# A decoder block in float32: the gate and up products of its SwiGLU by one level of Strassen's scheme

## The chip, the cores and the metric

The kernel runs on one core of one Trainium2 chip. The metric is the device time of one execution in microseconds (us), median of the runs. TensorE (PE) multiplies, VectorE (DVE), ScalarE (ACT) and GpSimd (POOL) do the elementwise work, SyncE (SP) issues every transfer between device memory and the on-chip memory SBUF; TensorE writes its products into PSUM, eight banks of 128 x 512 numbers.

## The reference

One decoder block over 1024 tokens of width 1024, all in float32:

```
mix = [norm(attention) | norm(pooling)] @ w_out
h   = x + norm(mix)
hn  = norm(h)                                              # 1024 x 1024
ff  = (silu(hn @ w_gate) * (hn @ w_up)) @ w_down           # 1024 -> 2816 -> 1024
h   = h + norm(ff)
out = h + sigmoid(h @ w_ple_gate) * norm(p @ w_ple)
```

The change concerns `hn @ w_gate`, `hn @ w_up`, and the work right before and after them.

## The kernel before

**Split operands.** Every factor of a large product is held as two parts, `hi + lo`, each of 12 significant bits. `split` (L102) makes them: ScalarE casts to `hi` (L104), VectorE subtracts to get `lo` (L105). `mm3` (L107) then issues three matmuls for each block of 128 x 128 by 128 x 512: hi by hi (L110), hi by lo (L111), lo by hi (L112).

**Order.** The kernel is written in Tile: buffers come from pools, a planner puts the instructions of each engine in an order by its own timing model, within the dependences, and places the semaphores. An instruction that waits holds back everything behind it on its engine. SP's queue is in order too. A pool lies at the left or the right end of SBUF's partitions (`side="right"`); pools of one side are stacked.

**The stages, in order.** Embedding, norm and the v projection (0 to 100 us); pooling mixer, q and k projections, attention (100 to 385 us); then the output projection: `pooled(t)` and `mixed(t)` for each of eight token tiles, and `rest(t)` (L579), which adds the residual, stores h, takes the second norm and transposes the tile into `h2T` (left side, hi and lo parts of 8 x 128 x 1024). Behind the last tiles, three products on the first half of the tokens run ahead (`early`, L601).

**The loop over the hidden width.** 2816 columns are 22 tiles of 128, in 11 chunks of two. For each tile, `ff_weights` loads 1024 x 128 of w_gate and w_up (512 KB each, pool `wg`, right side) and splits them; `ff_product` (L564) multiplies them with one half of the tokens, 8 blocks by 3 matmuls = 24 matmuls into one PSUM bank; `ff_half` (L620) takes Silu of the gate, multiplies it by up and splits the result (`f`, right side). When a chunk's two tiles are there, the down product runs over all eight token tiles and both halves of the output width, 96 matmuls, with the split rows of w_down (right side), and is added to `acc` by VectorE (L676). The next chunk follows.

**The end.** In the last chunk the loads and splits of w_ple_gate (`wpg`, left side) and the load of the last norm's gain into the one buffer `wd_raw` are issued. `hidden(t)` (L641) makes the norm of `acc`, adds it to h and transposes; `gated(t)` (L681) multiplies by `wpg` and writes the output.

## Time and profile before

| | us |
|---|---|
| median of 3 runs (1307.39 to 1310.54) | 1307.99 |
| span of the profiled execution, first to last instruction | 1305.0 |
| TensorE busy in it | 1279.1 |
| VectorE, ScalarE, GpSimd busy | 575.1, 421.0, 124.4 |

The profile gives a span and no time of its own execution; the span lies 3.0 us below the median of the runs. In the timeline a row has start, duration, engine, line, operation and the buffers written and read; the bracket at its end tells for how long the engine had been idle before it and what ended that. A matmul's duration (0.39 us) contains its way through the array, and the next one begins before it ends: the pace is the distance of two starts.

### The profile page before, as it was taken

What the parts mean: (1) busy time and instruction counts of PE and PEld (TensorE: products, weight loads), DVE (VectorE), ACT (ScalarE), POOL (GpSimd) and SP (SyncE); (2) the same over time, 40 slices, a digit from 0 to 9 for tenths busy, and PEclk for the clock granted to TensorE, in tenths of its full rate; (3) what the DMA queues carried; (4) which work ended last, traced back from release to release, by engine and by line L of the source; (5) the groups of instructions that cost most, each with busy time, mean ns of one, the idle gap of its engine ahead of it and who ended that gap; (6) DMA issues with size and microseconds to landing.
All of it is one profiled execution on the core that took longest, in us unless ns stands there. A gap on an engine that the chain in (4) does not pass through costs nothing.

```text
span 1305.0 us, 15784 instructions
## 1 busy us (share of the span) xinstructions
PE 1279.1 (98%) x6228; PEld 1051.4 (81%) x6228; DVE 575.1 (44%) x958; ACT 421.0 (32%) x790; POOL 124.4 (10%) x197
## 2 busy tenths in 40 slices
PE   8999999998999999999999999999999999998998
PEld 6898878887887878888888888888888888887887
DVE  6544635567674553133343333342424242417443
ACT  6533525567674543311111111212120212015211
POOL 2210200000014330000000000000000000007210
PEclk9999999999999999999999999999999999999999
DMA  9632495468515533111212121111111211124331
GB/s 301 213 101 74 151 278 152 137 192 229 139 36 186 159 104 97 48 51 34 63 33 65 33 65 33 53 44 50 36 62 33 65 33 54 44 68 142 105 121 65
DMA packets 107770, 128.77 MB, mean 99 GB/s; under 512 B 7792, under 2 KB 83376, under 8 KB 107696
## 3 DMA queue, kind: packets, MB, share of 16 engines
q1 hardware_dynamic: 107696, 127.76, 32.1%
q8 instruction: 49, 0.80, 0.3%
q14 instruction: 25, 0.20, 0.1%
HBM read 98.35 MB, written 29.39 MB: 98 GB/s over the span
## 4 chain that ended last, share of the span: by engine, by line
PE 89%; DMA 5%; ACT 2%; DVE 2%; issue 1%; POOL 1%; SPq 0%; DVEq 0%; ACTq 0%; POOLq 0%
PE ps_F L110 11%; PE ps_F L111 11%; PE ps_F L112 11%; PE ps_A L110 10%; PE ps_A L112 10%; PE ps_A L111 10%; PE ps_T L111 3%; PE ps_T L110 3%; PE ps_T L120 3%; PE ps_T L112 3%; PE ps_O L111 3%; PE ps_O L110 3%; PE ps_O L112 3%; PE ps_O L468 1%; PE ps_A L427 1%
## 5 line engine op out<-in xcount | busy, mean ns | idle before, releaser
L110 PE MATMUL ps_A<-h2T,wg_hi 128*128 128x512 f32 x352 | 139.0, 395 | 0.2 <-ACT h2T L104 0.2
L111 PE MATMUL ps_A<-h2T,wg_hi 128*128 128x512 f32 x352 | 138.8, 394 | 0.0
L110 PE MATMUL ps_F<-h2T,wg_hi 128*128 128x512 f32 x352 | 138.8, 394 | 0.0
L112 PE MATMUL ps_A<-h2T,wg_lo 128*128 128x512 f32 x352 | 138.7, 394 | 0.0
L112 PE MATMUL ps_F<-h2T,wg_lo 128*128 128x512 f32 x352 | 138.7, 394 | 0.0
L111 PE MATMUL ps_F<-h2T,wg_hi 128*128 128x512 f32 x352 | 138.7, 394 | 0.0
L623 DVE TENSOR_TENSOR sg<-ps_F,sg 128x512 f32<-128x512 f32 x44 | 30.4, 690 | 179.4 <-PE ps_F L112 179.4
L104 ACT CAST wd_hi<-wd_raw 128x1024 fp32r<-128x1024 f32 x22 | 23.1, 1051 | 251.1 <-PE ps_O L112 215.5
L104 ACT CAST wg_hi<-wg_raw 128x1024 fp32r<-128x1024 f32 x44 | 46.2, 1049 | 156.8 <-issue 77.9
L105 DVE TENSOR_TENSOR wg_lo<-wg_raw,wg_hi 128x1024 fp32r<-128x1024 f32 x44 | 55.6, 1263 | 84.3 <-ACT wg_hi L104 81.5
L676 DVE TENSOR_TENSOR acc<-ps_T,acc 128x512 f32<-128x512 f32 x80 | 55.2, 690 | 76.1 <-PE ps_T L112 76.0
L110 PEld LDWEIGHTS ps_A<-h2T,wg_hi 128*128 128x128 f32 x352 | 65.9, 187 | 16.4 <-ACT h2T L104 0.5
L111 PEld LDWEIGHTS ps_A<-h2T,wg_hi 128*128 128x128 f32 x352 | 65.9, 187 | 16.4 <-DVE h2T L105 0.4
L112 PEld LDWEIGHTS ps_F<-h2T,wg_lo 128*128 128x128 f32 x352 | 65.8, 187 | 16.3
L111 PEld LDWEIGHTS ps_F<-h2T,wg_hi 128*128 128x128 f32 x352 | 65.8, 187 | 16.2
L110 PEld LDWEIGHTS ps_F<-h2T,wg_hi 128*128 128x128 f32 x352 | 65.8, 187 | 16.2
L112 PEld LDWEIGHTS ps_A<-h2T,wg_lo 128*128 128x128 f32 x352 | 65.9, 187 | 16.1
L105 POOL TENSOR_TENSOR wpg<-wg_raw,wpg 128x1024 fp32r<-128x1024 f32 x3 | 7.4, 2471 | 703.8 <-ACT wpg L104 703.8
L676 DVE TENSOR_TENSOR acc<-ps_O,acc 128x512 f32<-128x512 f32 x80 | 55.2, 690 | 42.9 <-PE ps_O L112 42.8
L110 PE MATMUL ps_O<-wd_hi,f 128*128 128x512 f32 x176 | 68.6, 390 | 0.4 <-DVE acc L676 0.4
L111 PE MATMUL ps_T<-wd_lo,f 128*128 128x512 f32 x176 | 69.0, 392 | 0.0
L110 PE MATMUL ps_T<-wd_hi,f 128*128 128x512 f32 x176 | 68.7, 390 | 0.0
(265 smaller groups left out, 2813.2 us busy)
## 6 DMA issues: line engine op xcount, KB each, us to landing
wg_raw<-in_w_ffn_gate_dram SPq DMA_DIRECT2D x22, 512.0 KB, 4.0
wg_raw<-in_w_ffn_up_dram SPq DMA_DIRECT2D x22, 512.0 KB, 3.9
wd_raw<-in_w_ffn_down_dram SPq DMA_DIRECT2D x22, 512.0 KB, 3.6
xt<-in_x_dram SPq DMA_DIRECT2D x16, 512.0 KB, 5.0
wc_raw<-in_w_in_dram SPq DMA_DIRECT2D x12, 512.0 KB, 5.9
ed<-eo SPq DMA_DIRECT2D x8, 512.0 KB, 3.6
vd<-vs SPq DMA_DIRECT2D x8, 512.0 KB, 3.2
qs<-qd SPq DMA_DIRECT2D x8, 512.0 KB, 5.3
```

The costliest lines, as they stand in the source:

```text
L104: nc.scalar.copy(hi, raw)
L105: lo_by.tensor_tensor(out=lo, in0=raw, in1=hi.bitcast(F32), op=ALU.subtract)
L110: nc.tensor.matmul(ps, lh, rh, start=first, stop=False)
L111: nc.tensor.matmul(ps, lh, rl, start=False, stop=False)
L112: nc.tensor.matmul(ps, ll, rh, start=False, stop=last)
L120: nc.tensor.transpose(tp[:, j * P:(j + 1) * P], src[:, (c + j) * P:(c + j + 1) * P], ident)
L427: nc.tensor.matmul(ps[:, 0:n], qs[:, tok(i)], kh[:, c0:c1_], start=True, stop=False)
L468: nc.tensor.matmul(po[:, q0:W2], vh[:, j, :], pTs[1][:, j, q0:W2], start=False, stop=j == nj - 1)
L623: nc.vector.tensor_tensor(out=sg, in0=up, in1=sg, op=ALU.mult)
L676: nc.vector.tensor_tensor(out=acc[:, t, half(hf)], in0=ps, in1=acc[:, t, half(hf)], op=ALU.add)
```

## The change

The products A^T h for a gate or up weight are done on pairs of hidden tiles. A weight of 1024 x 256 is cut into quarters (two halves of the 1024 rows, two tiles of 128 columns), the transposed norm into quarters (two halves of the rows, two halves of the tokens), and the four quarter results come from seven products of quarters in place of eight, after Winograd's form of Strassen's scheme: four sums of weight quarters (S1 to S4, on GpSimd), four sums of token quarters (T1 to T4, made once), and seven sums of results, of which four are made by accumulating in PSUM and three by VectorE.

- One product of quarters is 4 blocks by 3 matmuls = 12 matmuls. There are 22 weights (`q`), 11 gate and 11 up, of seven products each.
- `rest(t)` no longer makes `h2T`. For tokens 0 to 511 it keeps both halves raw (`rw`) and splits them (B11, B21); for tokens 512 to 1023 it forms the differences on VectorE and GpSimd and splits B22. T1 to T4 are split after the last tile.
- Weights that meet B11, B21 and B22 (left side) lie on the left, in the place of the attention's result (`wl`); those that meet T1 to T4 (right side) lie on the right (`wr`, 4 buffers). For the first two weights all lie on the right.
- A weight pair is one load of 1 MB into one of two buffers (`wide`); the first two products (`first_two`) of the next weight are placed ahead of the last product of this one.
- The SwiGLU result is stored to a device buffer `ffd`, not kept. After the whole phase a second loop reads it back by 128 rows with w_down, splits both (pool `fd`, in the place of T1 to T4), and does the same down products as before. `wpg` and the gain `gfp` are loaded in that loop's third chunk and at its beginning.

```diff
-            transposed(tt, h2T[0][:, :, tok(t)], h2T[1][:, :, tok(t)], KT, "O")
+            if t < 4:
+                for c, name in enumerate(("B11", "B21")):
+                    nc.scalar.copy(rw[:, c, :, cols], tps[c])
+                    split(tps[c], hq[name][0][:, :, cols], hq[name][1][:, :, cols])
+            else:
+                r0, r1, r2, r3 = (rw[:, i, :, cols] for i in range(4))
+                nc.vector.tensor_tensor(out=r2, in0=tps[0], in1=r0, op=ALU.subtract)
+                nc.vector.tensor_tensor(out=r3, in0=tps[1], in1=r2, op=ALU.subtract)
+                split(tps[1], hq["B22"][0][:, :, cols], hq["B22"][1][:, :, cols])
+                nc.gpsimd.tensor_tensor(out=r0, in0=r3, in1=r0, op=ALU.subtract)
+                nc.gpsimd.tensor_tensor(out=r1, in0=r1, in1=r3, op=ALU.subtract)
...
-        ws = [ff_weights(w_gate, 0), ff_weights(w_up, 0), ff_weights(w_gate, 1)]
-        early = [ff_product(w, 0, tag) for w, tag in zip(ws, "AFA")]
...
+    psum_layout(Q=8)
...
+    def weights(raw, left):
+        a11, a21 = raw[:, 0:K2, 0:P], raw[:, 0:K2, P:2 * P]
+        a12, a22 = raw[:, K2:KT, 0:P], raw[:, K2:KT, P:2 * P]
+        def summed(x_, y_, op):
+            s = swp.tile([P, K2, P], F32, name="sw")
+            nc.gpsimd.tensor_tensor(out=s, in0=x_, in1=y_, op=op)
+            return s
+        out = {"A11": quarter_w(a11, left), "A12": quarter_w(a12, left)}
+        yield out
+        s1 = summed(a21, a22, ALU.add)
+        out["S1"] = quarter_w(s1, False)
+        s2 = summed(s1, a11, ALU.subtract)
+        out["S2"] = quarter_w(s2, False)
+        s4 = summed(a12, s2, ALU.subtract)
+        out["S4"] = quarter_w(s4, True)
+        s3 = summed(a11, a21, ALU.subtract)
+        out["S3"] = quarter_w(s3, False)
+        out["A22"] = quarter_w(a22, False)
+        yield out
...
+    def first_two(q):
+        q["a"], q["b"] = bank("Q"), bank("Q")
+        product(q["a"], q["w"]["A11"], "B11", True)
+        product(q["b"], q["w"]["A12"], "B21", True)
+
+    def middle(q):
+        a, b, w = q["a"], q["b"], q["w"]
+        p1 = temp()
+        nc.scalar.copy(p1, a)
+        c11 = temp()
+        nc.vector.tensor_tensor(out=c11, in0=b, in1=p1, op=ALU.add)
+        c = bank("Q")
+        product(c, w["S1"], "T1", True)
+        p5 = temp()
+        nc.scalar.copy(p5, c)
+        product(a, w["S2"], "T2", False)
+        u2 = p1
+        nc.scalar.copy(u2, a)
+        product(c, w["S4"], "B22", False)
+        c12 = u2
+        nc.vector.tensor_tensor(out=c12, in0=c, in1=u2, op=ALU.add)
+        product(a, w["S3"], "T3", False)
+        c22 = p5
+        nc.vector.tensor_tensor(out=c22, in0=a, in1=p5, op=ALU.add)
+        q["c"] = [c11, c12, None, c22]
+
+    def last(q):
+        product(q["a"], q["w"]["A22"], "T4", False)
+        q["c"][2] = q["a"]
...
+    for n in range(EARLY):
+        start(n)
+        first_two(qs[n])
+    for i, name in ((2, "T1"), (3, "T2"), (0, "T3"), (1, "T4")):
+        for k in range(0, K2, 2):
+            split(rw[:, i, k:k + 2, :], hq[name][0][:, k:k + 2, :], hq[name][1][:, k:k + 2, :])
+    lt = h2pool.tile([P, 16, HALF], F32, name="lt", tag="rw")
+    for n in range(NQ):
+        if n + 1 < NQ and n + 1 >= len(qs):
+            start(n + 1)
+        next(qs[n]["gen"])
+        middle(qs[n])
+        if n + 1 < NQ and n + 1 >= EARLY:
+            first_two(qs[n + 1])
+        last(qs[n])
+        if n % 2 == 0:
+            finish_gate(qs[n])
+        else:
+            finish_up(qs[n - 1], qs[n], n // 2)
...
+        def split_rows(f):
+            raw = wg.tile([P, 2, D], F32, name="fd_raw", tag="wide", bufs=2)
+            nc.sync.dma_start(out=raw[:, 0, :], in_=w_down[tok(f), :])
+            nc.sync.dma_start(out=raw[:, 1, :], in_=ffd[tok(f), :])
...
+            made = [split_rows(f) for f in range(f0, f0 + CHUNK)]
+            if f0 == 2 * CHUNK:
+                for k in range(0, KT, 2):
+                    raw = wg.tile([P, 2, D], F32, name="wpg_raw", tag="wide", bufs=2)
+                    nc.sync.dma_start(out=raw, in_=w_pg[k * P:(k + 2) * P, :].rearrange("(j q) c -> q j c", q=P))
+                    split(raw, wpg[0][:, k:k + 2, :], wpg[1][:, k:k + 2, :])
```

Here EARLY is 3, NQ is 22, K2 is 4, and `quarter_w` splits one quarter of a weight (4 x 128 columns) into hi and lo. `finish_gate` takes Silu of the four quarter results, `finish_up` multiplies them and stores them to `ffd`, 256 KB each.

## Rows read from the trace of the kernel before

**Rows 1.** The page: busy time, share of the span, instructions of TensorE
```profile
PE 1279.1 (98%) x6228; PEld 1051.4 (81%) x6228; DVE 575.1 (44%) x958; ACT 421.0 (32%) x790; POOL 124.4 (10%) x197
```

**Rows 2.** Windows: stretch, busy (count) of PE, PEld, DVE, ACT, POOL; clock; DMA; GB/s
```profile
620.00:800.00 180.00, 180.00 (x780) 145.74 (x779) 63.13 (x82) 27.66 (x36) 0.00 (x0) 1.00 0.16 47
1170.00:1206.00 36.00, 32.83 (x140) 25.79 (x138) 23.84 (x27) 17.42 (x25) 22.10 (x16) 0.95 0.42 146
1206.00:1305.00 99.00, 94.86 (x460) 77.99 (x460) 39.79 (x55) 20.50 (x36) 18.91 (x13) 1.00 0.29 96
```

**Rows 3.** Timeline of TensorE: first down matmul, second and eleventh chunk
```profile
577.38 0.39 PE L110 MATMUL ps_T<-wd_hi,f 128*128 128x512 f32 x1
...
1177.14 0.39 PE L110 MATMUL ps_T<-wd_hi,f 128*128 128x512 f32 x1
```

**Rows 4.** Timeline of TensorE: two gate/up matmuls, 24 matmuls apart
```profile
560.35 0.39 PE L112 MATMUL ps_A<-h2T,wg_lo 128*128 128x512 f32 x1
...
565.95 0.39 PE L112 MATMUL ps_F<-h2T,wg_lo 128*128 128x512 f32 x1
```

**Rows 5.** Timeline of TensorE: two matmuls of an input projection, 24 apart
```profile
109.59 0.39 PE L110 MATMUL ps_F<-hT,wc_hi 128*128 128x512 f32 x1
...
115.03 0.39 PE L110 MATMUL ps_A<-hT,wc_hi 128*128 128x512 f32 x1
```

**Rows 6.** Timeline of TensorE: two matmuls of the embedding, 5 apart
```profile
61.06 0.39 PE L110 MATMUL ps_F<-wpp,pT 128*128 128x512 f32 x1
...
62.19 0.39 PE L112 MATMUL ps_F<-wpp,pT 128*128 128x512 f32 x1
```

**Rows 7.** Groups by form, 500 to 1170 us: busy us, mean ns, idle before
```profile
L676 DVE TENSOR_TENSOR acc<-ps_T,acc 128x512 f32<-128x512 f32 x72 | 49.7, 691 | 76.0 <-PE ps_T L112 76.0
...
L105 DVE TENSOR_TENSOR wg_lo<-wg_raw,wg_hi 128x1024 fp32r<-128x1024 f32 x39 | 47.8, 1226 | 81.7 <-ACT wg_hi L104 79.2
...
L104 ACT CAST wg_hi<-wg_raw 128x1024 fp32r<-128x1024 f32 x39 | 40.9, 1049 | 150.0 <-issue 77.9 <-PE ps_A L111 72.1
...
L105 DVE TENSOR_TENSOR f<-sg,f 128x512 fp32r<-128x512 f32 x41 | 28.3, 689 | 15.1 <-ACT f L104 15.1
...
L104 ACT CAST f<-sg 128x512 fp32r<-128x512 f32 x41 | 25.4, 620 | 93.1 <-DVE sg L623 93.1
...
L622 ACT ACTIVATE sg<-ps_A 128x512 f32<-128x512 f32 x40 | 23.8, 595 | 52.2 <-PE ps_A L112 52.2
...
L674 ACT COPY acc<-ps_T 128x512 f32<-128x512 f32 x8 | 4.7, 588 | 9.8 <-PE ps_T L112 9.8
```

**Rows 8.** Groups by form, 400 to 485 us: the residual addition on GpSimd
```profile
L585 POOL TENSOR_TENSOR xt<-xt,pb 128x1024 f32<-128x1024 f32 x8 | 19.2, 2396 | 11.6 <-DVE pb L584 9.8 <-DMA xt<-in_x_dram 1.8
```

**Rows 9.** Timeline of ScalarE, 560 us: the copy behind the product of rows 4
```profile
560.84 0.60 ACT L622 ACTIVATE sg<-ps_A 128x512 f32<-128x512 f32 x1 [4.24 <-PE ps_A L112]
```

**Rows 10.** Timeline of VectorE and GpSimd around 457 us: two instructions that meet
```profile
457.47 2.87 DVE L105 TENSOR_TENSOR wg_lo<-wg_raw,wg_hi 128x1024 fp32r<-128x1024 f32 x1
...
456.85 2.41 POOL L585 TENSOR_TENSOR xt<-xt,pb 128x1024 f32<-128x1024 f32 x1 [1.40 <-DVE pb L584]
```

**Rows 11.** Timeline around 480 us: last token tile's norm, its transposes, the next product
```profile
478.23 1.27 DVE L588 SCALAR_TENSOR_TENSOR pb<-xt,h_r,gfr 128x1024 f32<-128x1024 f32 x1
...
481.08 1.03 PE L120 MATMUL ps_O<-ident,pb 128*128 128x128 f32 x8
482.36 0.50 PE L110 MATMUL ps_A<-h2T,wg_hi 128*128 128x512 f32 x1 [0.24 <-ACT h2T L104]
```

**Rows 12.** DMA issues: size of each, median us from issue to landing
```profile
wg_raw<-in_w_ffn_gate_dram SPq DMA_DIRECT2D x22, 512.0 KB, 4.0
```

**Rows 13.** Timeline around 1197 us: last down product, start of the gate
```profile
1196.19 1.28 DVE L648 SCALAR_TENSOR_TENSOR dn<-acc,y_r,wd_raw 128x1024 f32<-128x1024 f32 x1 [2.56 <-DMA wd_raw<-in_g_ffn_post_dram]
...
1197.33 0.39 PE L112 MATMUL ps_T<-wd_hi,f 128*128 128x512 f32 x1
...
1206.57 0.48 PE L112 MATMUL ps_A<-wpg,h 128*128 128x512 f32 x1
```

More of the change, by code (lines that the diff above doesn't have):

```diff
@@ L497, in block_kernel, with wide, narrow @@
     woa = pool(o_ctx, "woa", side="right")
-    wobs = [[wg.tile([P, D], F32R, name=f"wob{i}{k}", tag="wg_raw" if k == 3 else ("wg_hi", "wg_lo")[i],
-                     bufs=2 if k == 3 else 3) for k in range(4)] for i in range(2)]
+    def wide(name, bufs=2):
+        return wg.tile([P, 2, D], F32R, name=name, tag="wide", bufs=bufs)
+    def narrow(name):
+        return wg.tile([P, D], F32R, name=name, tag="wr", bufs=4)
+    wob01 = [wide(f"wob{k}") for k in range(2)]
+    wob23 = [[narrow(f"wob{i}{k}") for k in (2, 3)] for i in range(2)]
+    wobs = [[wob01[0][:, i, :], wob01[1][:, i, :], wob23[i][0], wob23[i][1]] for i in range(2)]
     woas = [woa.tile([P, 4, D], F32R, name=f"woa{i}") for i in range(2)]
@@ L554, in block_kernel, with quarter @@
     psum_layout(A=2, F=2, T=2, O=2)
-    def ff_weights(w, f):
-        raw = wg.tile([P, KT, P], F32, name="wg_raw", bufs=2)
-        nc.sync.dma_start(out=raw, in_=w[:, tok(f)].rearrange("(k q) c -> q k c", q=P))
-        hi = wg.tile([P, KT, P], F32R, name="wg_hi")
-        lo = wg.tile([P, KT, P], F32R, name="wg_lo")
-        split(raw, hi, lo)
-        return hi, lo
-    def ff_product(w, hf, tag):
-        ps = bank(tag)
-        for k in range(KT):
-            mm3(ps, (w[0][:, k, :], w[1][:, k, :]), (h2T[0][:, k, half(hf)], h2T[1][:, k, half(hf)]), k == 0, k == KT - 1)
-        return ps
+    K2 = KT // 2
+    hq = {}
+    def quarter(p, name):
+        hq[name] = [p.tile([P, K2, HALF], F32R, name=f"{name}{i}") for i in range(2)]
     h2_ctx = ExitStack()
     h2pool = pool(h2_ctx, "h2pool")
-    h2T = [h2pool.tile([P, KT, S], F32R, name=f"h2T{i}") for i in range(2)]
+    rw = h2pool.tile([P, 4, K2, HALF], F32, name="rw", tag="rw")
+    for name in ("B11", "B21", "B22"):
+        quarter(h2pool, name)
     with ExitStack() as c1:
@@ new lines, in block_kernel, with quarter_w @@
+    ffd = dram.tile([FF, S], F32, name="ffd")
+    psum_layout(Q=8)
+    g1_ctx = ExitStack()
+    cright = pool(g1_ctx, "cright", side="right")
+    swp = pool(g1_ctx, "swp", 5)
+    for name in ("T1", "T2", "T3", "T4"):
+        quarter(cright, name)
+    wl = apool.tile([P, 4, 2, K2, P], F32R, name="wl", tag="a_sb")
+    nl = [0]
+    def quarter_w(src, left):
+        if left:
+            w = wl[:, nl[0] % 4]
+            nl[0] += 1
+        else:
+            w = wg.tile([P, 2, K2, P], F32R, name="wr", tag="wr", bufs=4)
+        split(src, w[:, 0], w[:, 1])
+        return w
@@ new lines, in product, with temp @@
+    def product(ps, w, name, first):
+        for k in range(K2):
+            lh, ll, rh, rl = w[:, 0, k, :], w[:, 1, k, :], hq[name][0][:, k, :], hq[name][1][:, k, :]
+            for i, (l, r) in enumerate(((lh, rh), (lh, rl), (ll, rh))):
+                nc.tensor.matmul(ps, l, r, start=first and k == 0 and i == 0, stop=k == K2 - 1 and i == 2,
+                                 skip_group_check=not first)
+    late = [0]
+    def temp():
+        i = late[0] % 16
+        late[0] += 1
+        return lt[:, i, :]
@@ new lines, in last, with finish_gate, finish_up @@
+    def last(q):
+        product(q["a"], q["w"]["A22"], "T4", False)
+        q["c"][2] = q["a"]
+    def finish_gate(q):
+        q["sg"] = []
+        for i in (0, 1, 3, 2):
+            sg = q["c"][i] if i != 2 else temp()
+            nc.scalar.activation(out=sg, in_=q["c"][i], func=AF.Silu)
+            q["c"][i] = sg
+    def finish_up(g, u, f):
+        for i in (0, 1, 3, 2):
+            o = g["c"][i]
+            nc.vector.tensor_tensor(out=o, in0=u["c"][i], in1=g["c"][i], op=ALU.mult)
+            r0 = (2 * f + i // 2) * P
+            nc.sync.dma_start(out=ffd[r0:r0 + P, half(i % 2)], in_=o)
@@ new lines, in block_kernel, with start @@
+    NQ = 2 * (NF // 2)
+    EARLY = 3
+    qs = []
+    def start(n):
+        gen = weights(load_pair((w_gate, w_up)[n % 2], n // 2), n > 1)
+        q = {"w": next(gen), "gen": gen}
+        qs.append(q)
+    for n in range(EARLY):
[5 more added lines that the diff above has]
+    lt = h2pool.tile([P, 16, HALF], F32, name="lt", tag="rw")
```

117 lines of the change are left out of this document (51 added, 66 removed).

## The prediction

> **What bounds the kernel now.** I read the page first: TensorE is busy for 1279.1 of 1305.0 us [rows 1]. Busy time hides short stalls, since a matmul of 0.39 us overlaps its successor, so the windows by stage and then single distances come next. From 620 to 800 us TensorE is busy all the time and the other engines at most a third of it, GpSimd never [rows 2]. The loop has one rhythm: from the second to the eleventh chunk's first down matmul, nine chunks, 599.76 us pass [rows 3], 66.64 each. A chunk has 4 weights x 2 halves x 24 = 192 gate/up matmuls and 96 down matmuls. Two gate/up matmuls 24 apart lie 5.60 us apart [rows 4]: 0.2333 us each, 44.80 for 192. The remaining 21.84 give 0.2275 for a down matmul. So the loop is matmul pace and nothing else: only fewer or closer matmuls shorten it, and other engines' work is free while TensorE never waits for it.
>
> **The two paces.** In gate/up the weights lie on the right side, `h2T` on the left. In down both factors lie on the right, as in the input projections, where 24 matmuls take 5.44 us, 0.2267 each [rows 5]. In the embedding both lie on the left: five distances, 1.13 us, 0.226 [rows 6]. So either side alone is fast, the mixture slow. The Trainium skill ("TensorE: Matmul & The Clock Gate", Step-by-step: what each phase is for) says that TensorE has two independent read ports, so loading weights does not slow the running matmul. By that rule placement would be worth nothing. [rows 4 to 6] show 0.0066 us per matmul.
>
> **What the change takes away.** Gate/up loses 22 tiles x 96 = 2112 matmuls x 0.2333 = 492.8 us. It gets 22 weights x 7 products x 12 = 1848 matmuls. At 0.2275, the down pace, which I choose because there too splits and additions run alongside, that is 420.4; the first two weights meet B11, B21 and B22 across the sides, 72 matmuls x 0.0058 = 0.4. Saved: 492.8 - 420.8 = **72.0 us**. Bounds: 73.5 if all run at 0.2267; 61.6 if placement did nothing here and all ran at 0.2333 (431.2).
>
> **What the phase costs beside TensorE.** One weight is 84 x 0.2275 = 19.1 us of TensorE. ScalarE: seven quarter casts of 128x512 at 0.620, three PSUM copies at 0.588, half of four Silus at 0.595 [rows 7] = 7.3 us. VectorE: seven subtractions at 0.689, three result sums and half of four products at 0.691 [rows 7] = 8.3 us. GpSimd: four sums, half of 2.396 each [rows 8] = 4.8 us. All are covered by 19.1. GpSimd and VectorE can meet: the subtraction at 457.47 us took 2.87 us, while GpSimd added until 459.26 [rows 10], against 1.226 alone [rows 7]. The Trainium skill ("SBUF — State Buffer", Who interferes with whom) has VectorE instructions with two SBUF inputs block against GpSimd ones that read SBUF; the row agrees. If each of the four sums blocks one subtraction for its whole length, VectorE has 13.1 us, still below 19.1.
>
> The narrow place is PSUM. S2 T2 accumulates into the bank that the copy p1 reads, S4 B22 waits for the copy p5, S3 T3 for u2, and A22 T4 for the sum c22. p5 and u2 have one product, 12 x 0.2275 = 2.73 us, to hide in. The copy behind the product of [rows 4] began 0.10 us after its last matmul's end (560.35 + 0.39) [rows 9]; that matmul ends 0.16 us after the next could start. With 0.59 for the copy and 0.2 for the way back to TensorE (a guess: the 0.10 of the way there, doubled) about 1.05 us pass; 1.7 us are left for whatever stands ahead in ScalarE's queue, two casts. p1 and c22 have more (three and two products). I take 2 us in all; bounds 0 and 26 (1.2 us a weight).
>
> Loads: 1 MB a weight. 512 KB land in 4.0 us [rows 12]; twice that is 8. A `wide` buffer comes free when A22 two weights before is split, eleven products (30 us) before the data is needed, so this is covered. If not, the next `first_two` is late. The stores to `ffd` add 11.5 MB to SP's queue behind loads that wait; the 16 temporaries last over two weight pairs.
>
> **The start.** In before, the three early products, 72 matmuls or 16.8 us, fill the wait for the last token tile's norm: it ends at 479.5, its transposes start at 481.08, and the next product at 482.36 with 0.24 us lost [rows 11]. In after, the third weight's load must wait for the first weight's buffer, which is read until its A22 split, and that waits for a `wr` buffer that S1 T1 still reads. So only two weights, 48 matmuls, can run ahead: 5.6 us of cover are gone. Behind the transposes, T1 needs a subtraction (0.69), a cast of 1024 (1.05) and its subtraction (1.23) [rows 7], about 3.2 us with handovers where before 0.5 passed: 2.7. The GpSimd differences of the tiles before (2 x 1.2) can stand in front of that norm's GpSimd steps: 0 to 2.4, I take 1. The first weight's last product has no `first_two` ahead of it, so c22 shows: 1.1. Sum 10.4; I take 10. Bounds: 3, if products fill the gaps, and 18, if T2 to T4 (six more subtractions of 1.23 on VectorE) come in sequence as well.
>
> **The turn to down.** c22 shows again at the last weight (1.1). The f rows' lo parts lie where T4 lay, so two subtractions of 1.23 start only after the very last product, perhaps behind `finish_up`'s last product of 0.69. I take 4; bounds 2 and 10 (if the reading of `ffd` also waited for the last stores: a store and a load, some 4 us each by [rows 12]).
>
> **Down.** Per chunk TensorE 21.84; VectorE 16 x 0.691 + 4 x 1.226 = 16.0, GpSimd nothing. In the third chunk four `wpg` splits add 9.8 to VectorE, more than the chunk's room, but the next chunk has 5.8 spare and four PSUM banks buffer. I take 1; bounds 0 and 5.
>
> **The end.** In before, from 1197.33 to 1206.57 us [rows 13] TensorE does 7 down matmuls, 12 transposes (0.1 each) and 4 gate matmuls, 3.6 us of work in 9.2: 5.6 lost, while the gain's late load ends VectorE's wait at 1196.19 [rows 13] and the clock averages 0.95 [rows 2]. With `wpg` and gain there long before, the first `hidden` can run in the last chunk. I take a gain of 4.5; bounds 0 and 5.6. The rest of the gate stage keeps its sides and its pace.
>
> **The sum.** 1305.0 - 72.0 + 2 + 10 + 4 + 1 - 4.5 = 1245.5 us of span; plus the 3.0 us by which the runs' median lies above this profile's span: **1248 us**. All bounds at their best: 1305.0 - 73.5 + 0 + 3 + 2 + 0 - 5.6 + 3.0 = 1234.
>
> **Rivals.**
> 1. *The PSUM handovers bind.* ScalarE's queue is in order; a cast that waits for a late GpSimd sum holds up p5 or u2 behind it. For: GpSimd's instructions do meet VectorE's [rows 10]. Against: 7.3 of 19.1 us on ScalarE, and 1.7 us of room. Between 0.5 and 2 us a weight: 1257 to 1290.
> 2. *The same place, on the other side.* If p5, u2 and c22 all come late, each by 0.9 us more than its cover, a weight loses 2.7 us, 22 weights 59 us, and the time is about 1305: same; above that, slower. The point is 2.7 us a weight. For ScalarE to cause it, it must be 2.6 us late at p5 and u2 each time, with 62% of its time free; hence unlikely. At 3.5 us a weight: 1323.
> 3. *Placement does nothing.* If something else than the sides sets the pace, and all 1848 matmuls run at 0.2333 [rows 4], the time is 1248 + 431.2 - 420.8 = 1258. Against: three stages show the pairing [rows 4 to 6], none another one. The Trainium skill's two read ports speak for it, as said.
> 4. *The borders cost more.* Start and turn at their upper bounds together: +8 and +6, with a lower clock after longer idling: about 1263.
>
> **How the numbers follow.** The forecast (1236 to 1256) has 0.58, rival 1 0.14, rival 2 0.07 (0.03 of it same, 0.04 slower), rival 3 0.08, rival 4 0.10, and something better than 1236 0.03. 1248 is the likeliest case. For 8 in 10 the range reaches from the best bounds, 1234, to 1278: it holds the forecast, rivals 3 and 4 and the milder part of rival 1. Faster by over 0.3% (below 1304; 0.3% is about what a measurement here tells from no change): 0.93; within 0.3%: 0.03; slower: 0.04.
>
> **What would show it.** Right: 84 matmuls a weight at 0.2267 to 0.2283 us, weights 19.1 to 19.3 us apart, TensorE idle only at the start (some 10 us), the turn (4) and the end; the down chunks 21.9 us apart. Wrong: weights 20 us or more apart with TensorE released by ScalarE's copies; a pace of 0.2333; idle time before the products of the third weight or in the third down chunk.

## The result and the profile after

The changed kernel takes **1274.35 us** (median of 4 runs, 1271.23 to 1277.43) against 1307.69 us (1305.92 to 1310.54) for the kernel before on the same chip: ratio **0.975**, 95% interval 0.9725 to 0.9776. It is faster by 33 us; 60 had been forecast. Its profiled execution has a span of 1274.6 us, the forecast sum was 1245.5.

The page of the changed kernel: busy time and count of each engine, then the two groups of phase matmuls (busy, mean ns | idle before them). The line for [rows 1] comes first.

```profile
PE 1218.1 (96%) x5964; PEld 1009.6 (79%) x5964; DVE 713.5 (56%) x1124; ACT 502.5 (39%) x952; POOL 258.2 (20%) x289
...
L681 PE MATMUL ps_Q<-T,wr 128*128 128x512 f32 x1056 | 250.7, 392 | 5.9 <-ACT wr L104 4.2
...
L681 PE MATMUL ps_Q<-B,wl 128*128 128x512 f32 x744 | 176.3, 390 | 2.7 <-ACT wl L104 2.7
```

In a phase of more than 400 us TensorE idles for 8.6 us ahead of its products. Windows of TensorE by stage, the view of [rows 2]: stretch, busy (count), granted clock, DMA share, GB/s.

```profile
466.50:484.00 17.50, 2.24 (x11) 0.59 0.24 90
484.00:520.00 36.00, 27.25 (x101) 0.87 0.12 37
520.00:900.00 380.00, 380.00 (x1669) 1.00 0.25 83
900.00:950.00 50.00, 45.34 (x184) 0.93 0.38 137
950.00:1150.00 200.00, 200.00 (x885) 1.00 0.33 116
...
1190.00:1274.00 84.00, 78.81 (x381) 1.00 0.31 115
```

The steady phase and the down stage are full; what is missing lies at the start (466 to 520), at the turn (900 to 950) and, with 5.2 us, in the gate stage at the end. The chain that ended last has one unbroken piece of 1764 phase matmuls, with its start, length and count:

```profile
515.14 402.45 PE ps_Q L681 x1764
```

That is 0.2281 us each, against 0.2333 in [rows 4].

**The start.** Timeline of TensorE from the last mixed product on; in brackets the idle time before an instruction and what ended it.

```profile
464.23 0.39 PE L112 MATMUL ps_A<-woa,aT 128*128 128x512 f32 x1
465.73 1.06 PE L605 MATMUL ps_O<-ident,pb 128*128 128x128 f32 x8 [1.11 <-DVE pb L599]
475.61 1.94 PE L605 MATMUL ps_O<-ident,pb 128*128 128x128 f32 x8 [8.81 <-DVE pb L599]
484.93 1.94 PE L605 MATMUL ps_O<-ident,pb 128*128 128x128 f32 x8 [7.38 <-DVE pb L599]
486.52 13.09 PE L681 MATMUL ps_Q<-B,wr 128*128 128x512 f32 x48
503.80 1.22 PE L681 MATMUL ps_Q<-T,wr 128*128 128x512 f32 x2 [4.19 <-ACT wr L104]
...
515.14 1.26 PE L681 MATMUL ps_Q<-B,wl 128*128 128x512 f32 x4 [2.67 <-ACT wl L104]
```

From 464.46, when the next product could have begun, to 515.14 are 50.7 us. In them TensorE does 24 transposes (2.4 us at full clock) and 72 products (16.4): **31.9 us lost**. Waits make up 25.1 us of it (24.2 in the brackets shown, two short ones beside them); most of the rest is work at a lower clock, which is 0.59 from 466.5 to 484 us and 0.87 from there to 520: eight transposes take 1.94 us there in place of 1.06. In [rows 11] the same place lost 0.24 us. The 48 early products, which were to fill the wait for the last token tile, stand behind all transposes, and the transposes of one tile follow those of the tile before after more than 9 us.

**The turn to down.** TensorE, then ScalarE, then VectorE and SyncE's issue queue in the changed kernel:

```profile
931.25 0.79 PE L110 MATMUL ps_T<-wd_hi,f_hi 128*128 128x512 f32 x1 [2.86 <-ACT acc L805]
931.84 0.63 PE L111 MATMUL ps_T<-wd_lo,f_hi 128*128 128x512 f32 x1
...
936.96 0.56 PE L111 MATMUL ps_T<-wd_lo,f_hi 128*128 128x512 f32 x1
```
```profile
928.28 1.04 ACT L104 CAST wd_hi<-fd_raw 128x1024 fp32r<-128x1024 f32 x1 [7.72 <-DMA fd_raw<-in_w_ffn_down_dram]
...
930.62 0.58 ACT L805 COPY acc<-ps_T 128x512 f32<-128x512 f32 x1
```
```profile
923.20 1.22 DVE L105 TENSOR_TENSOR f_lo<-fd_raw,f_hi 128x1024 fp32r<-128x1024 f32 x1
...
924.44 0.33 SPq L780 DMA_DIRECT2D fd_raw<-in_w_ffn_down_dram  x1
```

ScalarE's copy of a finished sum stands behind a cast that waits for a transfer. That load was issued at 924.44, when VectorE's last split of the first row (923.20 to 924.42) had freed one of the two `wide` buffers; VectorE in turn began that row's splits only behind the last product, at 922.06. The stores of the last results had left SyncE 2 us earlier and did not hold it. Behind the wait 12 matmuls (931.84 to 936.96) start 0.427 us apart, the pace of the lower of the two clock levels (1.2 and 2.4 GHz), before 0.23 comes back.

**The end.** [rows 13] begin with the seventh down matmul from the last (the last one begins at 1199.39) and end with the first gate matmul behind twelve transposes, 9.2 us apart. The same two in the changed kernel are 5.2 us apart:

```profile
1167.39 0.39 PE L112 MATMUL ps_T<-wd_hi,f_lo 128*128 128x512 f32 x1
...
1172.57 0.48 PE L112 MATMUL ps_A<-wpg,h 128*128 128x512 f32 x1
```

But from the last down matmul to the end the changed kernel is no faster (105.8 us against 105.6): a token tile now takes 12.63 us (VectorE's first splits of two tiles begin at 1234.09 and 1246.72), 12.08 before (1269.78 and 1281.86). GpSimd's rows show why:

```profile
1203.33 2.39 POOL L817 TENSOR_TENSOR he<-he,dn 128x1024 f32<-128x1024 f32 x1 [9.38 <-DMA he<-h1d]
```

The residual sum waits for the load of `he`, one tile with two buffers for both `ht` and `et`.

### The profile page after: what moved, and what is told of

Read it like the earlier page. It is cut to its first block, busy times and chain, and to the rows that moved or that the text cites. A ratio compares the mean times of both kernels' runs of the same rounds, so it can differ in the third digit from the quotient of the medians.

```text
span 1274.6 us, 16032 instructions
## 1 busy us (share of the span) xinstructions
PE 1218.1 (96%) x5964; PEld 1009.6 (79%) x5964; DVE 713.5 (56%) x1124; ACT 502.5 (39%) x952; POOL 258.2 (20%) x289
## 4 chain that ended last, share of the span: by engine, by line
PE 84%; DMA 4%; DVE 4%; ACT 3%; POOL 2%; issue 2%; SPq 0%; POOLq 0%; DVEq 0%; ACTq 0%
PE ps_Q L681 32%; PE ps_F L110 5%; PE ps_F L111 5%; PE ps_F L112 5%; PE ps_A L110 4%; PE ps_A L112 4%; PE ps_A L111 4%; PE ps_T L110 3%; PE ps_T L111 3%; PE ps_T L112 3%; PE ps_T L120 3%; PE ps_O L111 3%; PE ps_O L112 3%; PE ps_O L110 3%; PE ps_A L428 1%
## 5 line engine op out<-in xcount | busy, mean ns | idle before, releaser
L681 PE MATMUL ps_Q<-T,wr 128*128 128x512 f32 x1056 | 250.7, 392 | 5.9 <-ACT wr L104 4.2
L681 PEld LDWEIGHTS ps_Q<-T,wr 128*128 128x128 f32 x1056 | 198.8, 189 | 50.9 <-ACT wr L104 4.6
L681 PE MATMUL ps_Q<-B,wl 128*128 128x512 f32 x744 | 176.3, 390 | 2.7 <-ACT wl L104 2.7
L681 PEld LDWEIGHTS ps_Q<-B,wl 128*128 128x128 f32 x744 | 139.5, 188 | 32.6 <-ACT wl L104 3.3
L105 DVE TENSOR_TENSOR wl<-w_raw,wl 128x512 fp32r<-128x512 f32 x40 | 54.7, 1390 | 48.7 <-ACT wl L104 48.6
L110 PE MATMUL ps_T<-wd_hi,f_hi 128*128 128x512 f32 x176 | 69.5, 395 | 3.4 <-ACT acc L805 2.9
L111 PE MATMUL ps_T<-wd_lo,f_hi 128*128 128x512 f32 x176 | 69.2, 393 | 1.0 <-DVE wd_lo L105 1.0
L112 PE MATMUL ps_T<-wd_hi,f_lo 128*128 128x512 f32 x176 | 69.1, 393 | 0.0
L111 PE MATMUL ps_O<-wd_lo,f_hi 128*128 128x512 f32 x176 | 69.0, 392 | 0.0
L112 PE MATMUL ps_O<-wd_hi,f_lo 128*128 128x512 f32 x176 | 69.0, 392 | 0.0
L110 PE MATMUL ps_O<-wd_hi,f_hi 128*128 128x512 f32 x176 | 68.9, 392 | 0.0
L92 POOL TENSOR_SCALAR y_ms<-y_ss 128x1 f32<-128x1 f32 x8 | 3.8, 472 | 274.7 <-ACT junk L99 274.5
L438 ACT ACTIVATE s_sb<-s_sb,mn 128x128 f32<-128x128 f32 (+3 forms) x64 | 50.0, 782 | 17.4 <-DVE mn L434 17.1
```

The costliest lines, as they stand in the source:

```text
L105: lo_by.tensor_tensor(out=lo, in0=raw, in1=hi.bitcast(F32), op=ALU.subtract)
L110: nc.tensor.matmul(ps, lh, rh, start=first, stop=False)
L111: nc.tensor.matmul(ps, lh, rl, start=False, stop=False)
L112: nc.tensor.matmul(ps, ll, rh, start=False, stop=last)
L438: nc.scalar.activation(out=s_sb[:, 0:nk], in_=s_sb[:, 0:nk], func=AF.Exp, scale=-1.0, bias=mx, accum_out=rsum)
L681: nc.tensor.matmul(ps, l, r, start=first and k == 0 and i == 0, stop=k == K2 - 1 and i == 2, skip_group_check=not first)
```

## The experiments

The table puts all kernels side by side. Its times are differences of starts in one profiled execution each: *mixed*, first to last product of the mixer's second half; *lag*, from that last product to the last scaling of rows (L599); *phase*, from that product to the first down matmul; *down*, first to last down matmul; *end*, from there to the end of the span. The ratio is to the kernel before, timed beside it, with its 95% interval; 0.001 is 1.3 us. The mixed stage begins between 382.5 and 390.1 us in these executions although no edit touches what stands ahead of it, so spans alone are not compared.

| kernel | mixed | lag | phase | down | end | ratio |
|---|---|---|---|---|---|---|
| changed | 75.8 | 18.2 | 457.0 | 247.5 | 105.8 | 0.9750 (0.9725 to 0.9776) |
| tags2 | 79.6 | 15.8 | 451.0 | 245.8 | 106.4 | 0.9741 (0.9720 to 0.9762) |
| layout | 95.7 | 12.2 | 449.7 | 247.2 | 105.9 | 0.9858 (0.9836 to 0.9881) |
| early2 | 75.8 | 18.3 | 451.8 | 245.7 | 105.6 | 0.9695 (0.9674 to 0.9716) |
| swap | 75.7 | 19.1 | 465.4 | 246.3 | 106.3 | 0.9803 (0.9781 to 0.9826) |
| e2_diff | 76.6 | 14.3 | 446.3 | 244.2 | 106.1 | 0.9651 (0.9628 to 0.9675) |
| e2_xt | 76.9 | 15.3 | 447.3 | 244.3 | 105.7 | 0.9656 (0.9630 to 0.9681) |
| e2_lt | 75.7 | 18.3 | 452.7 | 244.1 | 105.7 | 0.9701 (0.9668 to 0.9734) |
| e2_sums | 75.8 | 18.5 | 450.6 | 247.1 | 106.1 | 0.9698 (0.9683 to 0.9712) |
| e2_end | 75.7 | 18.4 | 453.0 | 241.9 | 102.3 | 0.9648 (0.9625 to 0.9670) |
| comb_a | 76.8 | 14.2 | 445.1 | 241.9 | 102.3 | 0.9611 (0.9595 to 0.9626) |
| comb_b | 81.2 | 11.2 | 445.2 | 241.9 | 102.3 | 0.9632 (0.9609 to 0.9654) |
| comb_c | 81.1 | 11.0 | 440.1 | 248.3 | 102.3 | 0.9629 (0.9607 to 0.9651) |

My first theory of the start was the order of the PSUM banks: that one ring's banks go out in program order, so that the early products come behind the last transposes. The rival was the serial chain of VectorE, GpSimd and ScalarE.

### early2: one early weight less

```diff
-    EARLY = 3
+    EARLY = 2
```

> Two weights instead of three have their first two products ahead of the phase; all else as in the changed kernel. Theory: TensorE's wait of 2.67 us at 515.14 for the cast of the third weight goes, and nothing else: 1 to 4 us less, 1270.5 to 1273.5. Rival: the third weight is late all the same, and the wait moves behind the first weight's products: no change, 1274 to 1275. With tags2 this tells what the bank order is worth by itself.

Ratio 0.9695, about 7 us less than the changed kernel, more than either text allowed. The wait for the third weight is gone as expected, the phase is 5.3 us shorter (2.67 of it this wait, 1.6 less at the products of the first weight), and the down stage is 1.8 shorter, which the edit does not touch: at the turn TensorE waited 2.27 us in place of 2.86, with 7 matmuls at half pace behind it in place of 12. So the early start of a third weight was a loss: its load cannot land in time, and TensorE has its first products in order ahead of work that is ready. The kernels below, but for layout and swap, build on it.

### tags2: the early products ahead of the last transposes

```diff
-    psum_layout(Q=8)
...
-        q["a"], q["b"] = bank("Q"), bank("Q")
+        q["a"], q["b"] = bank("A"), bank("F")
...
-        c = bank("Q")
+        c = bank("T")
...
-    EARLY = 3
+    EARLY = 2
...
-    psum_layout(A=2, F=2, T=2, O=2)
```

> The phase keeps the four pairs of PSUM banks of the stages around it (a in A, b in F, c in T) in place of one ring of eight, and two weights instead of three have their first two products ahead of the phase. Theory (order of the banks): the first products of weights 0 and 1 stood behind the transposes of the last token tile because banks of one ring are given out in program order; with banks of their own these 48 matmuls (about 11 us of TensorE) run as filler in the 31.8 us that were lost between 464.46 and 516.24, and the time falls by 9 to 16 us, to 1258 to 1265. Rival (serial chain): TensorE only waits for the norm chain and for the splits of T, and what fills the gap is taken from work that would have been ready anyway: below 3 us, 1271 to 1275. Second rival (handover): two banks for each of a, b and c are too few in the steady phase, and waits of up to 1 us per weight (22 weights) come up there; then the gain at the start is given back.

Ratio 0.9741: no gain over the changed kernel, and 6 us slower than early2, which is the fair comparison. The early products do move (the mixed stage is 3.8 us longer because they stand in it), and two banks each were enough in the steady phase. But TensorE then has nothing to do while the T splits run:

```profile
487.94 1.94 PE L605 MATMUL ps_O<-ident,pb 128*128 128x128 f32 x8 [8.62 <-DVE pb L599]
...
494.35 5.06 PE L680 MATMUL ps_T<-T,wr 128*128 128x512 f32 x11 [2.66 <-DVE T L105]
...
510.77 4.06 PE L680 MATMUL ps_T<-T,wr 128*128 128x512 f32 x10 [8.95 <-DVE wr L105]
```

Ahead of the transposes TensorE stands idle for 8.6 us where early2 has 17.4; behind them for 13.8, most of it for VectorE, where early2 has 3.5. **The theory of the bank order falls** as a cause of the loss; the serial chain remains.

### layout: the change of banks moved

```diff
+        tag = tag if tag in banks["bufs"] else "Q"
...
-    psum_layout(A=2, F=2, T=2, O=2)
+    psum_layout(Q=8)
...
-    psum_layout(Q=8)
```

> Control: only the place of the change of banks moves, from behind the mixer's last stage to ahead of its second half; every bank of that stage is then taken from the ring of eight too. Theory (order of the banks): one ring is still given out in program order, so the first products stay behind the last transposes: within 3 us of the changed kernel, 1271 to 1277. Rival (opening the new banks waits for the old ones to close): the first products move ahead of the transposes and 9 us or more come back, 1265 or less.

Ratio 0.9858, 14 us slower: neither text. It was no neutral control. With one ring for all purposes the mixed stage takes 95.7 us in place of 75.8; its products wait for ScalarE's casts of the transposed rows and then run 0.43 us apart at the lower clock:

```profile
466.07 0.80 PE L111 MATMUL ps_Q<-woa,aT 128*128 128x512 f32 x1 [3.96 <-ACT aT L105]
466.67 0.63 PE L112 MATMUL ps_Q<-woa,aT 128*128 128x512 f32 x1
467.09 0.63 PE L111 MATMUL ps_Q<-woa,aT 128*128 128x512 f32 x1
```

It says nothing on the early products; it does say that one ring for all purposes costs 20 us in the mixer's second half. (The phase behind it is 7 us shorter; what shortens it, no run isolates.)

### swap: both factors in opposite halves

```diff
-        out = {"A11": quarter_w(a11, left), "A12": quarter_w(a12, left)}
+        out = {"A11": quarter_w(a11, False), "A12": quarter_w(a12, False)}
...
-        out["S1"] = quarter_w(s1, False)
+        out["S1"] = quarter_w(s1, True)
...
-        out["S4"] = quarter_w(s4, True)
+        out["S4"] = quarter_w(s4, False)
```

(S2, S3 and A22 as S1.)

> Both factors of a product in opposite halves of the partition: A11, A12 and S4 go to the right buffers (their partners B11, B21, B22 are left), S1, S2, S3 and A22 to the left ones (their partners T1 to T4 are right). Theory (placement sets the pace, 0.2275 against 0.2333 us by the rows of before): the 1848 same-side matmuls of the changed kernel at 0.2281 go to 0.233 to 0.2335, 9 to 10.5 us more, 1283 to 1285. Rival (the pace of 0.2281 comes from the work itself, placement does nothing): within 2 us of the changed kernel, and the pace stays at 0.228. Second rival (the pace follows the side of the weight loads alone): A products keep one pace and T products the other, about half of the difference, 4 to 6 us.

Ratio 0.9803, about 7 us slower than the changed kernel. The timeline groups neighbouring matmuls of one kind; each starts where the one before ends its turn. A weight of the changed kernel, then one of swap:

```profile
720.45 5.61 PE L681 MATMUL ps_Q<-B,wl 128*128 128x512 f32 x24
725.90 2.92 PE L681 MATMUL ps_Q<-T,wr 128*128 128x512 f32 x12
728.67 2.89 PE L681 MATMUL ps_Q<-B,wl 128*128 128x512 f32 x12
731.40 8.36 PE L681 MATMUL ps_Q<-T,wr 128*128 128x512 f32 x36
739.60 5.61 PE L681 MATMUL ps_Q<-B,wl 128*128 128x512 f32 x24
```
```profile
703.87 5.76 PE L681 MATMUL ps_Q<-B,wr 128*128 128x512 f32 x24
709.47 2.96 PE L681 MATMUL ps_Q<-T,wl 128*128 128x512 f32 x12
712.27 2.96 PE L681 MATMUL ps_Q<-B,wr 128*128 128x512 f32 x12
715.07 8.42 PE L681 MATMUL ps_Q<-T,wl 128*128 128x512 f32 x36
723.32 6.00 PE L681 MATMUL ps_Q<-B,wr 128*128 128x512 f32 x25
```

19.15 us from one weight to the next become 19.45 here, 6.6 us for 22 weights; TensorE waits in neither stretch. So placement does set the pace, and rival 3 of the prediction falls. But the theory does not hold in full. In swap all B products go at 0.2333, as it says; of the T products shown the run of 12 does too, while the run of 36 goes at 8.25 / 36 = 0.229. Other weights of swap have it the other way round:

```profile
656.50 8.56 PE L681 MATMUL ps_Q<-T,wl 128*128 128x512 f32 x36
664.89 5.76 PE L681 MATMUL ps_Q<-B,wr 128*128 128x512 f32 x24
```

Here the matmuls of the run of 36 are 8.39 / 36 = 0.233 apart, those of the run of 12 behind it (670.49 to 673.25) 0.230. In the changed kernel the run of 12 T products is at 2.77 / 12 = 0.231, but that is not another pace of those products. The last 24 of the run of 36 that begins at 731.40 show it:

```profile
734.16 5.60 PE L681 MATMUL ps_Q<-T,wr 128*128 128x512 f32 x24
```

They take 5.44 / 24 = 0.2267 each, the 12 ahead of them 2.76 / 12 = 0.230: slow is what comes right behind the change from the left side to the right. So with both factors on one side, either one, the pace is the fast one, and the second rival (the side of the weights alone) falls too. With weights right and tokens left, as in the kernel before, it is 0.2333; with weights left and tokens right it lies between 0.229 and 0.233, and what decides there stays open.

### e2_diff and e2_xt: GpSimd's part of the mixer's last stage

e2_diff on top of early2:

```diff
-                nc.gpsimd.tensor_tensor(out=r0, in0=r3, in1=r0, op=ALU.subtract)
-                nc.gpsimd.tensor_tensor(out=r1, in0=r1, in1=r3, op=ALU.subtract)
+                nc.vector.tensor_tensor(out=r0, in0=r3, in1=r0, op=ALU.subtract)
+                nc.vector.tensor_tensor(out=r1, in0=r1, in1=r3, op=ALU.subtract)
```

> Two weights ahead of the phase, and the two differences r0 and r1 of each of the last four token tiles on VectorE instead of GpSimd. Theory (GpSimd is the late engine of the last stage of the mixer: 15.4 of the 18 us from 466 to 484 busy; per tile 2.35 for the sum, 2.45 for the two differences and 1.5 for the two norms): without the differences a tile takes 8.0 us again as before the change, in place of 8.8 to 9.3, and the wait of TensorE for VectorE's scaled rows falls from 17.4 to 12 to 15 us; 3 to 5 us less than early2, span 1259 to 1261. Rival (serial chain of norms, VectorE is as late): the differences only change engine, no change against early2, or up to 2 us more.

Ratio 0.9651, 5.7 us less than early2: the theory's side, a little more than it said. In the profiled executions the phase is 5.5 us shorter and the mixed stage 0.8 longer, which is the theory's 3 to 5; another 1.5 us come from the turn, where the clock did not fall this time, and no line of the edit bears on that:

```profile
920.12 0.50 PE L110 MATMUL ps_T<-wd_hi,f_hi 128*128 128x512 f32 x1 [2.34 <-ACT acc L805]
920.46 0.39 PE L111 MATMUL ps_T<-wd_lo,f_hi 128*128 128x512 f32 x1
```

GpSimd in early2, one token tile:

```profile
464.74 2.34 POOL L596 TENSOR_TENSOR xt<-xt,pb 128x1024 f32<-128x1024 f32 x1 [1.91 <-DVE pb L595]
467.05 1.26 POOL L616 TENSOR_TENSOR rw<-rw 128x512 f32<-128x512 f32 x1
...
469.61 0.19 POOL L92 TENSOR_SCALAR h_ms<-h_ss 128x1 f32<-128x1 f32 x1
```

The differences of one tile (L616, L617) stand between the residual sum and the norm (L92) of the next, 2.5 us each time. Without them the lag falls from 18.3 to 14.3 us and TensorE waits 13.5 us for the scaled rows in place of 17.4.

e2_xt adds:

```diff
-            nc.gpsimd.tensor_tensor(out=xt, in0=xt, in1=tt, op=ALU.add)
+            nc.vector.tensor_tensor(out=xt, in0=xt, in1=tt, op=ALU.add)
```

> As e2_diff, and the residual sum of 1024 columns on VectorE too, so that GpSimd has only the norms. Theory (GpSimd): the sum takes 1.2 to 1.4 us in place of 2.35, about 1.5 us less per tile for three tiles; the wait for the scaled rows falls to 8 to 11 us; another 3 to 5 us less than e2_diff, span 1255 to 1258. Rival (VectorE is as late): it now carries all of it beside the splits of B and of the first weights, and the time stays or rises by up to 3 us against e2_diff.

Ratio 0.9656: nothing on top, the rival. The lag is 15.3. What is left there reads as a chain of steps on three engines, not one late engine; no run takes it apart further.

### e2_sums: the weight sums on VectorE

```diff
-            nc.gpsimd.tensor_tensor(out=s, in0=x_, in1=y_, op=op)
+            nc.vector.tensor_tensor(out=s, in0=x_, in1=y_, op=op)
```

> As early2, with the sums S1 to S4 of the weights on VectorE instead of GpSimd; the differences r0 and r1 stay on GpSimd. It tells by what e2_diff gained. Theory (VectorE and GpSimd slow each other when they meet at the T splits): without the sums on GpSimd only r0 and r1 of the last tile meet the T splits; the eight splits' median falls from 1744 ns to 1213, but VectorE has four more instructions of 0.69 there: 1 to 4 us less than early2. Rival (the differences gained in the norm chain alone, tile by tile): nothing or up to 3 us more than early2, and the wait for the scaled rows stays at 17.4 us. In both the steady phase keeps its pace of 0.2281: VectorE has 8.3 + 2.8 = 11.1 of 19.1 us per weight.

Ratio 0.9698: the rival, no change against early2. The T splits, minimum / median / maximum in ns, in early2 and in e2_sums:

```profile
L105 DVE TENSOR_TENSOR T<-rw,T x8: 1210/1744/2333, 484.4 to 498.0; 128x1024 fp32r<-128x1024 f32 x8
```
```profile
L105 DVE TENSOR_TENSOR T<-rw,T x8: 1208/1211/2325, 487.3 to 499.2; 128x1024 fp32r<-128x1024 f32 x8
```

Most of the collisions do go, but VectorE's added instructions take the place of what they cost. So e2_diff gained mainly by the norm chain: the lag stays 18.5 here. (In e2_diff the eight splits are at 1213 too, with no more work on VectorE at that point than the last tile's two differences.)

### e2_lt: the copies out of PSUM freed from the T splits

```diff
-    rw = h2pool.tile([P, 4, K2, HALF], F32, name="rw", tag="rw")
+    rw = [h2pool.tile([P, K2, HALF], F32, name=f"rw{i}", tag=f"rw{i}") for i in range(4)]
...
-    lt = h2pool.tile([P, 16, HALF], F32, name="lt", tag="rw")
+    lts = [h2pool.tile([P, 4, HALF], F32, name=f"lt{i}", tag=f"rw{i}") for i in (2, 3, 0, 1)]
```

> Two weights ahead of the phase, and the buffer of the partial results in four pieces, each over one quarter of the raw differences, so that the first copy out of PSUM waits for two of the eight T splits and not for all. Theory: ScalarE's wait of 6.7 us at its first copy goes, the cast of S2 that stands behind it is 6 us earlier, and TensorE's wait of 3.5 us for S2's low half goes to below 1 us: 2.5 to 4 us less than early2, span 1260 to 1261.5. Rival (VectorE's queue of T splits is what is late, S2's low half stands behind them anyway): the copy moves, TensorE waits as long, within 1 us of early2.

Ratio 0.9701, no change: the rival. The copy does move, to 492.66 us, the cast of S2 behind it to 493.14. TensorE still waits 4.0 us for S2's low half, because in VectorE's queue that stands behind the last four T splits:

```profile
493.68 5.71 DVE L105 TENSOR_TENSOR T<-rw,T 128x1024 fp32r<-128x1024 f32 x4
499.31 0.68 DVE L105 TENSOR_TENSOR wr<-sw,wr 128x512 fp32r<-128x512 f32 x1
```

### e2_end: the turn and the end

```diff
-                        nc.scalar.copy(acc[:, t, half(hf)], ps)
+                        nc.vector.tensor_copy(acc[:, t, half(hf)], ps)
...
-            he = wg.tile([P, 2, D], F32, name="he", tag="wide", bufs=2)
-            ht, et = he[:, 0, :], he[:, 1, :]
+            ht = fd.tile([P, D], F32, name="ht", tag="wd_hi")
+            et = fd.tile([P, D], F32, name="et", tag="wd_lo")
```

> Two weights ahead of the phase; at the turn to the down product the copies of the first chunk's sums out of PSUM are on VectorE instead of ScalarE; in the gate stage at the end the two loads of a token tile have four buffers each instead of two together. Theory, turn: TensorE's wait of 2.3 us for ScalarE's copy goes, and the half clock behind it with it: first to last down matmul 245.7 to 242.5 us or less. Theory, end: a tile takes 12.1 to 12.3 us as before the change in place of 12.63, 2 to 4 us less from the last down matmul to the end (105.6). Rival, turn: VectorE is at its own subtractions of the down rows, which wait for the same transfers, and the wait only changes its name. Rival, end: the pace is set by the transposes and splits of the next tile between the products, not by the loads: no change.

Ratio 0.9648, 6 us less than early2, both theories: down from 245.7 to 241.9, end from 105.6 to 102.3. The wait for the copy is gone, and the granted clock from 900 to 950 us is 1.00. A token tile of the gate stage takes 12.08 us again, as these two splits of h3 in e2_end show:

```profile
1174.13 0.68 DVE L105 TENSOR_TENSOR h<-ps_T,h 128x512 fp32r<-128x512 f32 x1
...
1186.21 0.68 DVE L105 TENSOR_TENSOR h<-ps_T,h 128x512 fp32r<-128x512 f32 x1
```

### comb_a, comb_b, comb_c: together

comb_a is early2 with the edits of e2_diff and e2_end; comb_b adds the banks of tags2; comb_c adds the four buffers of e2_lt to comb_b.

> All three edits that gained by themselves, together: two weights ahead of the phase, the differences r0 and r1 on VectorE, the first chunk's copies on VectorE with more buffers for the loads of the gate stage. Theory (three separate places: start, turn, end): the gains add, early2 7 us, e2_diff 5.6 and e2_end 6 less than the changed kernel's 1274: ratio to the kernel before 0.9600 to 0.9615, 1255 to 1257, span 1254 to 1256. Rival (they share VectorE or fluctuations of the runs make up part of each): ratio 0.963 or more.

> As comb_a, with the banks of tags2: the first products of weights 0 and 1 (48 matmuls, 11 us) stand between the last mixed products and the last transposes. Theory (VectorE's chain was the limit in tags2: its 8 T splits took 17 us beside GpSimd, 10.3 us with the differences moved): now T1 is ready some 5 us after the last transposes, TensorE has nothing else to do then, and the T products start 3 to 6 us earlier than in comb_a: ratio 0.956 to 0.959. Rival (the splits of the sums S1 to S4 stand behind those of T in VectorE's queue, and the early products delay the last tiles of the mixer as in tags2, where the last mixed product ended 79.6 us behind the first, in place of 75.8): no gain, up to 5 us more than comb_a.

> comb_b with the partial results' buffer in four pieces as in e2_lt. In comb_b TensorE waited 6.3 us, until 498.22, for ScalarE's first copy out of PSUM, which waits for the last of the eight T splits because its destination lies over the raw differences. Theory (early products help once nothing behind them waits for all T splits): the copy waits for T1 only, S2 T2 starts at about 492, and 4 to 6 us of comb_b come back: ratio to the kernel before 0.9585 to 0.960, 1252.5 to 1255, as good as comb_a or up to 3 us better. Rival (the T splits themselves are late: 8 x 1.21 us on VectorE and its other work from 484.7 to 497.5): TensorE waits for T2 to T4 one by one in place of the copy, less than 2 us come back, ratio 0.962 or more, and the early products are worth nothing in any order.

**comb_a** takes 1255.05 us (1253.9 to 1258.34), ratio 0.9611 (0.9595 to 0.9626): the gains add as forecast, and it is the fastest of all, 52 us below the kernel before and some 18 below the changed one. **comb_b** is no better (0.9632): the phase is as long, the mixed stage 4.3 us longer, as its rival said. **comb_c** removes the wait on which comb_b hung, and the phase is 5.1 us shorter, as its theory said. The total does not follow (0.9629): in the profiled execution the down stage is 6.4 us longer, because the turn comes out otherwise. TensorE, then VectorE, in comb_c:

```profile
919.39 0.80 PE L110 MATMUL ps_T<-wd_hi,f_hi 128*128 128x512 f32 x1 [3.85 <-DVE acc L803]
```
```profile
917.51 1.23 DVE L105 TENSOR_TENSOR wd_lo<-fd_raw,wd_hi 128x1024 fp32r<-128x1024 f32 x1 [3.68 <-ACT wd_hi L104]
918.65 0.68 DVE L803 COPY acc<-ps_T 128x512 f32<-128x512 f32 x1
```

The copies are on VectorE as in e2_end, but now one split of a row that waits for its transfer stands ahead of them, as the rival of e2_end had it. So e2_end's gain at the turn came from the place in a queue, not from the engine. Set against comb_a, comb_c's early products cost 4.3 us in the mixed stage and give 5.0 back in the phase: even without that wait they are worth about nothing. Waits of 5.0 us for a T split and of 2.3 for a later copy remain in it.

## Why the prediction was right, and where it missed

The direction, the mechanism of the gain and the range (1234 to 1278) held. The forecast itself (1236 to 1256) did not: the time lies 26 us above 1248, and only 4 us inside the range. That the range held is in part luck. Its upper part was room for rival 1, waits for the copies out of PSUM, which did not come; start, turn, down and end all at their worst bounds give 1248.5 + 8 + 6 + 4 + 4.5 = 1271, and the borders cost more than that. The 29.1 us between the forecast span and the measured one are all at the borders.

**What it takes away: right.** 1776 phase matmuls, from 515.14 to 921.25 less one wait of 0.8, are 405.3 us, 0.2282 each against 0.2275; for all 1848 that is 421.7 in place of 420.8. Weights are 19.15 us apart, in the forecast's 19.1 to 19.3. The cross-side products of the first two weights were 48, not 72 (their S4 lies on the left, other than the description of the change has it); that is 0.1 us. Of the 71 us that this gives, some 7 are the placement's by swap; the rest are the matmuls that are not done.

**The phase beside TensorE: right.** Of the 2 us taken for the PSUM handovers the steady phase shows none. VectorE, ScalarE and GpSimd are covered; GpSimd's sums slow VectorE's subtractions (for `wl` 1390 ns on average; 684 in e2_sums, where the sums are on VectorE), and it costs nothing there. Rivals 1 and 2 fall: no copy releases TensorE in 402 us.

**The start: the step that failed.** I took 10, with bounds 3 and 18; 31.9 were lost. Three of its parts were wrong.
- "So only two weights, 48 matmuls, can run ahead: 5.6 us of cover are gone." All cover was gone, since none of the 48 ran ahead of the last transposes. tags2 and comb_c show that this alone cost little: moved ahead, the products leave as much idle time behind the transposes.
- GpSimd's differences: "0 to 2.4, I take 1". They came between the steps of every tile's norm. The lag was 18.2 us where [rows 11] with the last mixed product of before (465.57) give 12.7. e2_diff got 4 of these 5.5 back, and 5.5 us in the phase.
- The T splits were at their upper bound and beyond. I had them in sequence, six more at 1.23; eight took 13.7 us, slowed by GpSimd, and behind them stood the split of S2. e2_lt shows that this queue, not the copy out of PSUM, is what was late.

Nor was the clock in the sum, some 6 us of the 31.9; the 1.1 us for c22 do not show here. The third weight was forecast rightly not to be ready; that the kernel issues its first products ahead of ready work, at 2.67 us and in all some 5 (early2), was not in the sum. The reason I gave for its late load was half wrong: it waits for the first weight's A22 split, but the buffer that this split needs is freed by the second weight's first products, not by S1 T1.

With comb_a the phase takes 445.1 us, so 12 of the 20.7 us by which it was longer than forecast are recovered. What is left there are above all two waits of 6.57 and 6.88 us for the scaled rows of the last two tiles, which no experiment removed.

**The turn: right in kind, mis-sized.** I took 4 (bounds 2 and 10). c22 shows with 0.79 us and the low part of the first row with 1.01, as described. What I had not followed is what those late splits hold up in turn: they free the buffers of the next loads, and in ScalarE's queue the copies stand behind the cast of such a load. That wait of 2.86 us and the 12 matmuls at half pace were not in the sum; with them the turn cost some 8 us (0.8, and 247.5 - 240.2 in the down stage).

**Down: right.** The 200 us from 950 are full; the four `wpg` splits cost nothing.

**The end: the forecast gain of 4.5 was made and given back.** The passage to the gate is 4.1 us shorter. But `ht` and `et` share one tile with two buffers, where before each had its own, and every token tile grew by 0.55 us. I had read only the passage and assumed that the rest "keeps its sides and its pace"; with buffers of their own (e2_end) 3.3 us of the gain are there.

By the table: the phase from the last mixed product to the first down matmul was forecast at 2.4 + 420.8 + 2 + 10 + 1.1 = 436.3 and took 457.0 (+20.7); down at 1056 x 0.2275 + 2.9 + 1 = 244.1, took 247.5 (+3.4); the end at 105.6 - 4.5 = 101.1, took 105.8 (+4.7). These add up to 28.8; they divide the 29.1 only to a microsecond or two, since the three forecasts come to 1.6 us more than the forecast span leaves behind the mixer, and the mixer itself ended 1.3 us earlier than before. Rival 4, costlier borders, is the one that came, with 29 in place of 14.

## What to carry to other kernels

When a loop is made shorter by moving work into a preparation, price the preparation as a chain: follow the last input through every engine's queue to the first product, with each instruction of the tiles before that stands in those queues, and ask what fills TensorE until then. An instruction that waits for a transfer holds up everything behind it on its engine, whichever engine that is, so look at what stands behind it rather than at how busy the engine is. And where the change merges two buffers into one, read the pace of each stage that uses them, not only the passage into it.
